# Keeping the split-off low parts of the projection weights in DRAM between the two halves of a decoder layer

## Chip, cores and metric

The kernel runs on one core of a Trainium2 chip. A core has five engines, each with an instruction queue that runs in order: TensorE (PE: matmuls; its weight loads, PEld, are listed apart), VectorE (DVE), ScalarE (ACT), GpSimd (POOL) and SyncE (SP), which here only issues DMAs. The engines wait for each other through semaphores. The time is the device time of one launch in microseconds (us), the median of the runs.

## What is computed

One decoder layer on 1024 tokens of 1024 channels, in float32. What matters here is the first step: the normalised input is multiplied with one wide weight matrix, and its columns feed two mixers.

```python
h = _rms_norm(x, norm_pre_mix[i])
...
p = h @ w_in.astype(h.dtype)
u = p[..., :GLU_COLS]
q = p[..., GLU_COLS:]
q = q + (_token_shift(q) - q) * mu.astype(h.dtype)
...
y = _wkv7(r_h, decay.reshape(B, T, H, N), k_h, v_h, -kk, kk * a_h)
...
c = u[..., :D_CONV] * jax.nn.sigmoid(u[..., D_CONV:])
c = _causal_dwconv(c, cconv_w, cconv_b)
c = jax.nn.silu(_layer_norm(c, cln_g, cln_b))
mix = jnp.concatenate([rwkv_out, c], axis=-1) @ w_out.astype(h.dtype)
```

`_wkv7` is a recurrence over the tokens with a state per head (8 heads of 64), `_causal_dwconv` a convolution over 31 tokens. The layer ends with a feed-forward part of 2816 hidden channels.

## The kernel before

**Precision.** TensorE multiplies in a float32 format with fewer bits than float32 (F32R). So that the result is still a float32 one, each operand is split: the high part `hi` is the value cast to F32R, the low part `lo` is the value minus `hi`. A product is then three matmuls: `wh` with `hi`, `wh` with `lo`, `wl` with `hi`. `split` (L155) makes the two parts of a weight: a cast on ScalarE and a subtraction on GpSimd or VectorE (GpSimd up to the last matrix, `low_pool`).

**Two halves.** The mixer runs over the tokens in two halves of 512 (`h` is 0 and 1 in `mixer`, L1073). `project` (L301) makes one block of 128 columns for one half. A block's weights come as two pieces of 128x512 (256 KB). For each piece `weight` (L160) issues a DMA from `w_in` into `wr` (three buffers), lets ScalarE cast it into `wh` (two buffers) and GpSimd subtract into `wl` (two buffers); then twelve matmuls use it. The 20 blocks of `w_in` are made in `rkv_in` (12: r, k and v) and `glu_in` (8: value and gate of the convolution); two narrower ones, `w_wa` and `w_g`, in `wa_in` and `gate_in`. All of it is done once for each half: the weights of the second half are loaded, cast and subtracted again, 40 pieces of `w_in` in each half.

**What surrounds it.** While the projections of one half run, the other work of the mixer goes on: `conv` (L392) adds 31 shifted products per block on VectorE into a PSUM bank (tile `pc`, L401), `conv_norm` (L403) normalises them (L412 to L417 on VectorE, the power of L153 on GpSimd, transposes and a silu, L422), `elementwise` (L426) prepares decay and keys of a quarter of the tokens (L443 to L498 on VectorE and ScalarE), `scores` (L504), `keys`, `inverses`, `merge` and `recurrence` (L669) make the recurrence. Behind the second half's projections come `w_out`, the feed-forward part's norm (`norm_ffn`, L822) and its matmuls.

**What sets the order.** The program is written as streams with priorities; a scheduler lays the instructions of all streams on the five engines before the launch, by its own model of their durations. On the chip each engine follows that order. `high_priority` in `weight` puts the load, the cast and the subtraction ahead of what its stream has pending. All DMAs of the kernel stand in SyncE's one queue.

Of the kernel before, what the change touches and what calls it, by code (L numbers as in the profile page):

```python
# [12 lines left out]
F32 = mybir.dt.float32  # L13
# [8 lines left out]
P = 128  # L22
# [72 lines left out]
class Trunk:  # L95
# [61 lines left out]
        eng = self.nc.gpsimd if pool else self.nc.vector  # L157
        return self.nc.scalar.copy(hi, src), eng.tensor_tensor(lo, src, hi.bitcast(F32), ALU.subtract)  # L158

    def weight(self, src, shape, home=None, held=None):  # L160

        with self.tc.high_priority():
            raw = (self.f2p.tile(shape, F32, tag="f2", name=self.nm("wr")) if held is self.hp else
                   self.wp.tile(shape, F32, tag="wr", bufs=3, name=self.nm("wr")))
            self.nc.sync.dma_start(raw, src)
            if held:
                hi, lo = self.pair("w", held)
            elif home:
                hi, lo = (home[0].tile(shape, F32R, tag=t, bufs=BUFS[t], name=self.nm("wm")) for t in home[1:])
            else:  # L170
                hi, lo = (self.wp.tile(shape, F32R, tag=t, bufs=2, name=self.nm(t)) for t in ("wh", "wl"))
            self.low = self.split(hi, lo, raw, self.low_pool)[1]
        return hi, lo


    def setup(self):
        nc, tc, ctx, a = self.nc, self.tc, self.ctx, self.a
        pool = lambda name, **kw: ctx.enter_context(tc.tile_pool(name=name, bufs=1, **kw))
        self.cp = pool("const")
        self.small = ctx.enter_context(tc.tile_pool(name="small", bufs=4))  # L180
        self.wp = ctx.enter_context(tc.tile_pool(name="wp", bufs=1))
        self.hp = ctx.enter_context(tc.tile_pool(name="hp", bufs=2 * KT))
        self.dp = pool("dram", space=DRAM)
        self.rowp = pool("rowp")
        cp = self.cp
        self.params = cp.tile([P, NPAR], F32, name="params")
        self.const = cp.tile([P, NCONST], F32, name="const")
        with self.stream("first"):
            nc.sync.dma_start(self.const[:, :P], a["consts"][:, :P])
        nc.sync.dma_start(self.params, a["params"])  # L190
        nc.sync.dma_start(self.const[:, P:], a["consts"][:, P:])
        self.mhalf = cp.tile([P, 8], F32, name="mhalf")
        nc.gpsimd.memset(self.mhalf, -0.5)
        self.mixd = self.dp.tile([SEQ, D], F32, name="mixd")
        self.early = self.dp.tile([EARLY - KEPT, P, HALF], F32, name="early")
        self.x1d = self.dp.tile([SEQ, D], F32, name="x1d")
        self.ssq = cp.tile([P, 8, 4], F32, name="ssq")
        self.sums = self.dp.tile([4, HT, P, 512], F32, name="sums")
        self.ecarry = cp.tile([P, 2, EARLY, 2], F32, name="ecarry")

# [97 lines left out]
            nc.vector.tensor_scalar(row[1], row[1], ss[:, 3:4], None, ALU.mult)  # L298


    def project(self, src, m, hs, halves=False):  # L301


        ps = self.bank()
        if halves:
            ws = [self.weight(src[j], [P, 4, m]) for j in range(2)]
            for ts in (slice(0, 256), slice(256, 512)):
                for k in range(KT):
                    (wh, wl), (hi, lo) = ws[k // 4], hs[k]
                    self.mm(ps[:m, ts], wh[:, k % 4], hi[:, ts], start=k == 0, stop=False)  # L310
                    self.mm(ps[:m, ts], wh[:, k % 4], lo[:, ts], start=False, stop=False)
                    self.mm(ps[:m, ts], wl[:, k % 4], hi[:, ts], start=False, stop=k == KT - 1)
            return ps
        for j in range(2):
            wh, wl = self.weight(src[j], [P, 4, m])
            for kk in range(4):
                hi, lo = hs[4 * j + kk]
                first, last = j == 0 and kk == 0, j == 1 and kk == 3
                self.mm(ps[:m], wh[:, kk], hi, start=first, stop=False)
                self.mm(ps[:m], wh[:, kk], lo, start=False, stop=False)  # L320
                self.mm(ps[:m], wl[:, kk], hi, start=False, stop=last)
        return ps
# [32 lines left out]
    def rkv_in(self, h, hs, st, name):  # L355
        name, pp = name
        j = "rkv".index(name)
        if name == "v":
            t = self.tl("v", [P, 2, HALF])
        else:  # L360
            t = self.row("row", 4).rearrange("p (l t) -> p l t", l=2)
        for l in range(2):
            i = 4 * j + 2 * pp + l
            ps = self.project(self.a["w_in"][i], P, hs, h == 0 and name == "k" and pp == l == 0)
            self.shift(ps, t[:, l], POFF["mu_r"] + i, h)
        st[name, pp] = t

    def glu_in(self, h, hs, st, i):

        nc, a = self.nc, self.a  # L370
        ps2 = self.project(a["w_in"][16 + i], P, hs)
        c = self.tl("c", [P, CONV_W - 1 + HALF])
        with self.tc.high_priority():
            nc.scalar.activation(c[:, CONV_W - 1:], ps2, AF.Tanh, scale=0.5)
        ps1 = self.project(a["w_in"][12 + i], P, hs)
        if h == 0:
            nc.gpsimd.memset(c[:, :CONV_W - 1], 0.0)
        else:
            nc.gpsimd.tensor_copy(c[:, :CONV_W - 1], self.ccarry[:, i])
        with self.tc.high_priority():  # L380
            if h == 0 and i == 3:

                t = self.tl("t2", [P, HALF])
                nc.scalar.copy(t, ps1)
                ps1 = t
            nc.vector.scalar_tensor_tensor(c[:, CONV_W - 1:], c[:, CONV_W - 1:], 1.0, ps1, ALU.add, ALU.mult)
        if h == 0:
            nc.gpsimd.tensor_copy(self.ccarry[:, i], c[:, HALF:])
        st["c", i] = c
# [683 lines left out]
    def mixer(self, sts):  # L1073
# [95 lines left out]
        self.R = self.tl("r", [P, NH, CH])  # L1169
        nc.vector.memset(self.R[64:128], 0.0)  # L1170
        project(0, hs, "k0 w k1 r0 r1")
        with self.stream("norm"):
            two = self.tl("mixr", [P, 2, D])
# [3 lines left out]
            with tc.issue_after(self.mark_hi.ins), tc.issue_after(self.mark_lo.ins):  # L1177
                self.norm_rows(rows)
        weave(quarter(0))
        project(0, hs, "v0 v1 g")  # L1180
        prepare(0)
        project(0, hs, "u0 u1")
        conv(0, 0)
        conv(0, 1, W[0].mark)
# [116 lines left out]
```

## Time and profile before

| | us |
|---|---|
| median of 3 runs (1321.29 to 1322.49) | 1321.41 |
| the profiled execution | 1319.54 |
| its span, first to last instruction | 1317.8 |

The mean granted clock of TensorE in the profiled execution is 0.988 of full speed. The page's slices cut the span into 40 of 33 us; a digit is the busy share in tenths:

```profile
PE   6999989999899989999999899999999999999996
DVE  5276998997799979995531364355555438479566
ACT  6553664567755765556642474443333445544451
POOL 4343433343443322444463466676666540000001
DMA  6222211121124351222354765656564433335326
```

The mixer's first half takes about the first 5 slices, the second half the projections of slices 6 to 11 and the work behind them up to slice 19; the rest is the feed-forward part. A busy share says how long an engine works, not who waits for it; who waits is read from the chain of waits and from the idle time that a row of the order in time shows in brackets, with the engine that ended it.

### The profile page before, as it was taken

To read this page: it belongs to the slowest core of one execution; us is meant where nothing else is said; L and a number is where in the kernel's file an instruction comes from. 1 tells how busy PE (TensorE), PEld (TensorE's weight loads), DVE (VectorE), ACT (ScalarE), POOL (GpSimd) and SP (SyncE) were. 2 spreads that over 40 slices of the span, in tenths; PEclk is the share of its full clock that TensorE was granted. 3 is DMA by queue.
4 is the path that set the end of the run, shared out by engine and by line. 5 is a ranking of instruction groups with operands and counts; after the bars stand their busy time and mean duration, and the time that the engine had idled before them with its cause. 6 is when DMAs were issued, how large, how long until landed. Compare 5 with 4: busy or idle time off the path is not lost.

```text
span 1317.8 us, 22852 instructions
## 1 busy us (share of the span) xinstructions
PE 1259.8 (96%) x8580; PEld 1015.9 (77%) x8580; DVE 877.9 (67%) x1520; ACT 680.0 (52%) x1354; POOL 515.3 (39%) x452
## 2 busy tenths in 40 slices
PE   6999989999899989999999899999999999999996
PEld 4777767777679967787789688888888888888884
DVE  5276998997799979995531364355555438479566
ACT  6553664567755765556642474443333445544451
POOL 4343433343443322444463466676666540000001
PEclk9999999999999989999999999999999999999998
DMA  6222211121124351222354765656564433335326
GB/s 216 81 79 63 66 49 49 42 74 57 49 77 105 119 167 46 68 71 67 102 151 134 257 204 186 192 170 207 170 195 145 122 94 112 97 112 160 104 65 207
DMA packets 85647, 155.79 MB, mean 118 GB/s; under 512 B 9280, under 2 KB 15808, under 8 KB 85536
## 3 DMA queue, kind: packets, MB, share of 16 engines
q1 hardware_dynamic: 85536, 154.33, 38.4%
q8 instruction: 67, 1.10, 0.4%
q14 instruction: 44, 0.36, 0.1%
HBM read 129.13 MB, written 25.17 MB: 117 GB/s over the span
## 4 chain that ended last, share of the span: by engine, by line
PE 72%; DVE 15%; ACT 4%; DMA 3%; issue 3%; POOL 2%; SPq 1%; POOLq 0%; ACTq 0%; DVEq 0%
PE pb L131 60%; DVE pc L401 4%; PE pe L131 4%; PE pn L131 3%; PE xs L131 3%; POOL wl L158 1%; DVE dw L578 1%; DMA x<-x1d 1%; ACT wh L158 1%; DVE pt L470 1%; DVE nrow L962 1%; DMA wr<-ffn_up 1%; PE pe L146 1%; DVE kk L471 1%; DVE h L265 1%
## 5 line engine op out<-in xcount | busy, mean ns | idle before, releaser
L158 POOL TENSOR_TENSOR wl<-wr,wh 128x512 fp32r<-128x512 f32 (+1 forms) x280 | 369.9, 1322 | 439.6 <-ACT wh L158 413.1
L131 PE MATMUL pb<-f,wh 128*128 128x512 f32 x1408 | 442.4, 395 | 2.5 <-ACT pb L773 1.8
L158 ACT CAST wh<-wr 128x512 fp32r<-128x512 f32 (+1 forms) x319 | 195.9, 615 | 331.1 <-PE pb L131 171.8
L131 PEld LDWEIGHTS pb<-f,wh 128*128 128x128 f32 x1408 | 263.5, 188 | 61.9 <-ACT pb L773 2.0
L131 PE MATMUL pb<-f,wl 128*128 128x512 f32 x704 | 280.0, 398 | 2.7 <-POOL wl L158 2.7
L131 PE MATMUL pb<-h,wh 128*128 128x512 f32 (+3 forms) x720 | 229.4, 398 | 2.0 <-ACT wh L158 1.4
L879 DVE SCALAR_TENSOR_TENSOR acc<-pb,params,acc 128x511 f32<-128x511 f32 (+1 forms) x128 | 95.4, 745 | 183.5 <-ACT acc L874 123.9
L401 DVE SCALAR_TENSOR_TENSOR pc<-c,params,pc 128x512 f32<-128x512 f32 x232 | 174.0, 750 | 4.7 <-ACT pc L398 0.5
L131 PEld LDWEIGHTS pb<-f,wl 128*128 128x128 f32 x704 | 132.4, 188 | 37.2 <-POOL wl L158 6.6
L131 PEld LDWEIGHTS pb<-h,wh 128*128 128x128 f32 (+2 forms) x720 | 131.7, 188 | 34.3 <-ACT wh L158 3.3
L131 PE MATMUL pb<-h,wl 128*128 128x512 f32 (+3 forms) x360 | 146.2, 406 | 3.0 <-POOL wl L158 2.9
L153 POOL TENSOR_TENSOR ss<-var,mhalf 128x1 f32<-128x1 f32 x16 | 11.0, 694 | 230.1 <-DVE ss L943 203.3
L131 PE MATMUL pb<-w,a 128*128 128x512 f32 x366 | 89.8, 393 | 0.0
L131 PEld LDWEIGHTS pb<-h,wl 128*128 128x128 f32 (+2 forms) x360 | 67.8, 188 | 22.2 <-POOL wl L158 5.6
L131 PE MATMUL pb<-wh,a 128*128 128x512 f32 x240 | 81.5, 396 | 0.0
L131 PEld LDWEIGHTS pb<-w,a 128*128 128x128 f32 x366 | 68.7, 188 | 16.1
L879 DVE SCALAR_TENSOR_TENSOR pt<-pb,params,pt 128x511 f32<-128x511 f32 (+1 forms) x48 | 35.7, 744 | 33.7 <-ACT ecarry L876 33.2
L919 POOL TENSOR_TENSOR b<-b,b 128x512 f32<-128x512 f32 x44 | 57.1, 1298 | 0.9
L131 PEld LDWEIGHTS pb<-wh,a 128*128 128x128 f32 x240 | 45.1, 188 | 10.6
L874 ACT ACTIVATE acc<-pb,params 128x512 f32<-128x512 f32 x64 | 49.5, 774 | 1.8 <-PE pb L131 1.8
L131 PE MATMUL pb<-wl,a 128*128 128x512 f32 x120 | 47.7, 397 | 0.0
L158 DVE TENSOR_TENSOR a<-act,a 128x512 fp32r<-128x512 f32 x50 | 33.3, 687 | 18.4 <-ACT a L158 18.3
(300 smaller groups left out, 2017.0 us busy)
## 6 DMA issues: line engine op xcount, KB each, us to landing
wr<-ffn_up SPq DMA_DIRECT2D x176, 256.0 KB, 2.7
wr<-w_in SPq DMA_DIRECT2D x80, 256.0 KB, 2.6
b<-ffn_down SPq DMA_DIRECT2D x44, 256.0 KB, 3.9
sums<-b SPq DMA_DIRECT2D x44, 256.0 KB, 2.7
wr<-sums SPq DMA_DIRECT2D x44, 256.0 KB, 2.7
wr<-ffn_down SPq DMA_DIRECT2D x33, 256.0 KB, 2.7
wr<-w_out SPq DMA_DIRECT2D x32, 256.0 KB, 2.7
mixd<-t SPq DMA_DIRECT2D x16, 256.0 KB, 3.2
```

The source lines that it names most:

```text
L131: return self.nc.tensor.matmul(out, lhsT, rhs, start=start, stop=stop, skip_group_check=skip)
L146: self.nc.tensor.transpose(out, in_, self.con("ident")[:n, :n])
L158: return self.nc.scalar.copy(hi, src), eng.tensor_tensor(lo, src, hi.bitcast(F32), ALU.subtract)
L265: self.mark_lo = nc.vector.scalar_tensor_tensor(lo[:, toks], pv, g, hi[:, toks].bitcast(F32), ALU.mult, ALU.subtract)
L401: nc.vector.scalar_tensor_tensor(out, c[:, j:j + HALF], w(j), acc, ALU.mult, ALU.add)
L470: nc.vector.tensor_tensor_scan(sg[:, l], self.con("scan"), sg[:, l], 0.0, ALU.mult, ALU.add)
L471: nc.vector.scalar_tensor_tensor(kk[:, l], k[:, l], self.par("k_k", 2 * pp + l), kk[:, l], ALU.mult, ALU.mult)
L578: nc.vector.tensor_tensor(dv[:, j + 1:, :j], dv[:, j + 1:, :j], tv, ALU.add)
L874: nc.scalar.activation(acc, ps, AF.Identity, scale=w(2), bias=self.par("fb", ch))
L879: nc.vector.scalar_tensor_tensor(acc[:, o:], ps[:, :HALF - o], w(j), acc[:, o:], ALU.mult, ALU.add)
L919: sub = lambda o, x, y, op=ALU.subtract: nc.gpsimd.tensor_tensor(o, x, y, op)
L962: nc.vector.tensor_tensor(out, a, b, op)
```

## The change

`weight` gets a further argument, `kept`: a flag for the half, and a place in a new DRAM tensor `lows` (20 blocks of two pieces). In the first half it works as before, and then a DMA stores the low part into `lows`. In the second half ScalarE still casts the high part out of the loaded `wr`, but the low part comes by a DMA from `lows` into `wl`, and GpSimd's subtraction is left out. `w_wa` and `w_g` stay as they were, and so do all other weights. The low parts are the same bits as before.

```diff
-    def weight(self, src, shape, home=None, held=None):
+    def weight(self, src, shape, home=None, held=None, kept=None):
...
-            self.low = self.split(hi, lo, raw, self.low_pool)[1]
+            if kept and kept[0]:
+                self.nc.scalar.copy(hi, raw)
+                self.nc.sync.dma_start(lo.bitcast(F32), kept[1])
+            else:
+                self.low = self.split(hi, lo, raw, self.low_pool)[1]
+        if kept and not kept[0]:
+            self.nc.sync.dma_start(kept[1], lo.bitcast(F32))
         return hi, lo
...
+        self.lows = self.dp.tile([20, 2, P, 4, P], F32, name="lows")
...
-    def project(self, src, m, hs, halves=False):
+    def project(self, src, m, hs, halves=False, kept=None):
...
+        low = lambda j: kept and (kept[0], self.lows[kept[1], j])
...
-            ws = [self.weight(src[j], [P, 4, m]) for j in range(2)]
+            ws = [self.weight(src[j], [P, 4, m], kept=low(j)) for j in range(2)]
...
-            wh, wl = self.weight(src[j], [P, 4, m])
+            wh, wl = self.weight(src[j], [P, 4, m], kept=low(j))
...
-            ps = self.project(self.a["w_in"][i], P, hs, h == 0 and name == "k" and pp == l == 0)
+            ps = self.project(self.a["w_in"][i], P, hs, h == 0 and name == "k" and pp == l == 0, (h, i))
...
-        ps2 = self.project(a["w_in"][16 + i], P, hs)
+        ps2 = self.project(a["w_in"][16 + i], P, hs, kept=(h, 16 + i))
...
-        ps1 = self.project(a["w_in"][12 + i], P, hs)
+        ps1 = self.project(a["w_in"][12 + i], P, hs, kept=(h, 12 + i))
```

The scheduler lays the whole program anew. SyncE's queue had 573 rows and has 653, GpSimd's had 453 and has 413. Three places follow; the numbers in the names are the buffers', and lines from L158 on stand up to nine lines later in the changed kernel.

SyncE, in the second half's projections of the convolution's blocks (about 317 to 340 us of the profile before), before: one load of a raw piece after the other.

```order
L165 DMA wr_3461<-w_in 128x512
L165 DMA wr_3479<-w_in 128x512
L165 DMA wr_3500<-w_in 128x512
L165 DMA wr_3518<-w_in 128x512
L165 DMA wr_3539<-w_in 128x512
L165 DMA wr_3557<-w_in 128x512
```

The same pieces in the changed kernel, with the loads of low parts between them:

```order
L166 DMA wr_3502<-w_in 128x512
L175 DMA wl_3466<-lows 128x512
L166 DMA wr_3520<-w_in 128x512
L166 DMA wr_3541<-w_in 128x512
L175 DMA wl_3484<-lows 128x512
L175 DMA wl_3505<-lows 128x512
L166 DMA wr_3559<-w_in 128x512
L175 DMA wl_3523<-lows 128x512
L166 DMA wr_3580<-w_in 128x512
L175 DMA wl_3544<-lows 128x512
L166 DMA wr_3598<-w_in 128x512
L175 DMA wl_3562<-lows 128x512
```

A piece's low part (`wl_3523` belongs to `wr_3520`) stands behind the raw load of the piece two to three later. In the first half the stores stand in the same way, each behind the raw load of a piece three or four later.

GpSimd, about 325 to 349 us, before: `XG` is the recurrence's, `mv` and `gn` are powers of the two normalisations.

```order
L158 TENSOR_TENSOR wl_3482<-wr_3479,wh_3481 128x512
L691 TENSOR_TENSOR XG_3855<-r_3788,GE_1163 64x256
L153 TENSOR_TENSOR mv_3203<-var_3205,mhalf 128x1
L158 TENSOR_TENSOR wl_3503<-wr_3500,wh_3502 128x512
L158 TENSOR_TENSOR wl_3521<-wr_3518,wh_3520 128x512
L153 TENSOR_TENSOR gn_3694<-var_3700,mhalf 128x8
L158 TENSOR_TENSOR wl_3542<-wr_3539,wh_3541 128x512
L691 TENSOR_TENSOR XG_3858<-r_3788,GE_1163 64x256
L158 TENSOR_TENSOR wl_3560<-wr_3557,wh_3559 128x512
L153 TENSOR_TENSOR mv_3226<-var_3228,mhalf 128x1
```

The same stretch in the changed kernel:

```order
L700 TENSOR_TENSOR XG_3896<-r_3829,GE_1188 64x256
L153 TENSOR_TENSOR mv_3244<-var_3246,mhalf 128x1
L153 TENSOR_TENSOR gn_3735<-var_3741,mhalf 128x8
L700 TENSOR_TENSOR XG_3899<-r_3829,GE_1188 64x256
L153 TENSOR_TENSOR mv_3267<-var_3269,mhalf 128x1
```

The subtractions are gone and the rest keeps its order.

VectorE, about 353 to 360 us, before: scores (L525, L526), the recurrence's sum (L710) and the last tile of the convolution's normalisation (L412 to L417).

```order
L525 TENSOR_TENSOR l_590_3721<-pe_3724,const 128x4x64
L526 TENSOR_TENSOR ca_3722<-pe_3724,const 128x4x64
L710 TENSOR_TENSOR r_3846<-xs_94,XG_3855 64x256
L710 TENSOR_TENSOR r_3846<-xs_95,XG_3858 64x256
L412 BN_STATS bs_3247<-pc_3242 128x6
L725 TENSOR_REDUCE gn_3899<-mixr_1959 128x8
L414 BN_AGGR mv_3249<-bs_3247 128x2
L386 SCALAR_TENSOR_TENSOR c_3536<-c_3536,pb_3538 128x512
```

And in the changed kernel, from the same score on:

```order
L534 TENSOR_TENSOR l_590_3762<-pe_3765,const 128x4x64
L535 TENSOR_TENSOR ca_3763<-pe_3765,const 128x4x64
L719 TENSOR_TENSOR r_3887<-xs_95,XG_3896 64x256
L395 SCALAR_TENSOR_TENSOR c_3577<-c_3577,pb_3579 128x512
L534 TENSOR_TENSOR l_590_3762<-pe_3779,const 128x4x64
L535 TENSOR_TENSOR ca_3778<-pe_3779,const 128x4x64
L534 TENSOR_TENSOR l_590_3762<-pe_3780,const 128x4x64
L535 TENSOR_TENSOR ca_3778<-pe_3780,const 128x4x64
L719 TENSOR_TENSOR r_3887<-xs_96,XG_3899 64x256
L421 BN_STATS bs_3288<-pc_3283 128x6
```

The gate's product (L386) and the next four score products now stand ahead of the normalisation's last tile. Up to here VectorE's order is that of before; from here on it differs in several places, up to about 640 us.

## Prediction

> **What bounds the kernel now.** I read the page's busy shares and slices first, then the chain of waits cut into stretches, then the waits by engine, and last the order in time of the stretch where the removed work lies.
>
> ```profile
> PE 1259.8 (96%) x8580; PEld 1015.9 (77%) x8580; DVE 877.9 (67%) x1520; ACT 680.0 (52%) x1354; POOL 515.3 (39%) x452
> PE 72%; DVE 15%; ACT 4%; DMA 3%; issue 3%; POOL 2%; SPq 1%; POOLq 0%; ACTq 0%; DVEq 0%
> L158 POOL TENSOR_TENSOR wl<-wr,wh 128x512 fp32r<-128x512 f32 x40 | 54.0, 1352 | 89.4 <-ACT wh L158 74.2 <-PE pb L131 8.6 <-ACT r L700 3.4
> ```
>
> TensorE sets the time: 96% busy, 72% of the chain. GpSimd is 39% busy, on 2% of the chain. The third row is what the change takes away: 40 subtractions of 1.352 us, 54.0 us on GpSimd, counted in the stretch 181 to 380 us where the second half's projections run. An engine with 2% of the chain cannot return 54 us. The question is where those 40 held somebody else.
>
> ```profile
> 181.00:312.00 131.00, 125.63 (x1352) 97.26 (x1346) 120.38 (x209) 72.14 (x144) 47.07 (x45) 0.97 0.19 52
> 312.00:362.00 50.00, 45.98 (x363) 35.44 (x362) 37.01 (x66) 40.30 (x83) 22.18 (x22) 1.00 0.18 52
> 362.00:460.00 98.00, 93.99 (x1026) 83.22 (x1025) 93.16 (x162) 60.03 (x127) 38.13 (x32) 0.98 0.36 98
> by line: PE pb L131 58.0%; PE pe L131 13.5%; PE xs L131 10.1%; DVE pc L401 5.2%; PE pe L146 3.3%; DVE h L265 2.5%; PE xs L146 1.8%; PE Y L131 1.6%; DVE l L495 0.8%; DVE pt L494 0.8%; DVE pt L498 0.6%; DVE l L489 0.5%; PE pb L146 0.5%; DVE c
> by line: PE pb L131 36.2%; issue 8.3%; PE pe L131 7.0%; ACT co L422 5.6%; POOL wl L158 5.6%; PE xs L131 4.2%; ACT wh L158 3.8%; PE pc L146 3.7%; ACT kk L448 3.2%; ACT L422 2.6%; ACT L473 2.6%; ACT L474 2.6%; ACT pt L492 2.2%; ACT pt L465 1.
> by line: DVE pc L401 30.9%; PE pb L131 8.7%; DVE dw L578 5.6%; issue 5.3%; DVE m L158 4.8%; DVE t L767 3.2%; DVE v L335 2.6%; DVE sub L576 2.6%; DVE pt L470 2.3%; DVE l L534 2.3%; DVE dw L567 2.2%; DVE l L590 2.1%; DVE pt L468 2.0%; DVE kk
> ```
>
> The first three rows give busy time of PE, PEld, DVE, ACT, POOL in three stretches; the next three are the chain's shares in the same stretches. From 181 to 312 the chain is TensorE's own work, so freeing GpSimd there returns almost nothing. From 312 to 362 it passes from TensorE to ScalarE, VectorE and GpSimd, and TensorE stands idle for 4 of 50 us: this is the only stretch where the low parts are on the chain. From 362 to 460 VectorE is 95% busy and is the chain; it starts when the stretch before ends, so a gain made by 362 is carried on.
>
> **The removed subtractions.** They cost in two ways: TensorE waits for a low part, and VectorE is held while GpSimd subtracts.
>
> ```profile
> PEld pb L131 <- POOL wl L158: 1.8, 2, 1.1
> PE pb L131 <- POOL wl L158: 0.9, 2, 0.6
> L401 DVE SCALAR_TENSOR_TENSOR pc<-c,params,pc 128x512 f32<-128x512 f32 x91 | 68.4, 752 | 2.0
> L498 DVE SCALAR_TENSOR_TENSOR pt<-row,params,pt x16: 472/485/1519, 76.1 to 463.2; 128x256 f32<-128x256 f32 x16
> 325.25 1.71 POOL L158 TENSOR_TENSOR wl<-wr,wh 128x512 fp32r<-128x512 f32 x1 [6.01 <-ACT wh L158]
> 326.34 1.16 DVE L489 SCALAR_TENSOR_TENSOR l<-kk,pt 128x512 f32<-128x512 f32 x1
> 325.13 0.69 DVE L488 SCALAR_TENSOR_TENSOR kk<-pt,kk 128x512 f32<-128x512 f32 x1
> 330.47 2.71 POOL L158 TENSOR_TENSOR wl<-wr,wh 128x512 fp32r<-128x512 f32 x2
> 331.26 2.20 DVE L498 SCALAR_TENSOR_TENSOR pt<-row,params,pt 128x256 f32<-128x256 f32 x2
> 335.21 0.63 ACT L473 ACTIVATE pt<-pt 128x512 f32<-128x512 f32 x1 [2.29 <-DVE pt L470]
> 343.44 0.50 PE L131 MATMUL pb<-h,wl 128*128 128x512 f32 x1 [0.63 <-POOL wl L158]
> ```
>
> Waits first: in the whole stretch TensorE's matmuls wait 0.9 us for low parts and its weight loads 1.8, partly the same time. Then holding: the convolution's step at L401, which adds into PSUM, takes 752 ns throughout, but L498, with two SBUF operands, takes 485 at the median and up to 1519 ns. Both long cases in 330 to 335 lie inside GpSimd's pair of subtractions.
>
> The Trainium skill, page "SBUF — State Buffer", section "SBUF: two separate sides", says that VectorE and GpSimd share one port pair under an exclusive lock, and that only VectorE operations with two SBUF inputs or in a two-port mode are caught. By that rule the 68.4 us of L401 gain nothing from an idle GpSimd, and the trace agrees with its steady 752 ns; if every VectorE step were slowed, the sum below would be several times larger.
>
> *Term 1, 325 to 344 us.* L489 takes 1.16 us where its neighbour of the same shape, L488, takes 0.69: 0.47 lost. The two L498 take 2.20 where two medians make 0.97: 1.23 lost. Together 1.70 us, ahead of the scan L470 for which ScalarE waits 2.29 us, so ScalarE gets all of it. Its in-order work then leads to the cast for which TensorE waits (next fence), and TensorE's wait of 0.63 us for that piece's low part goes too: 2.33 us.
>
> ```profile
> 338.98 0.44 PE L146 MATMUL pc<-const,co 128*128 128x128 f32 x2 [0.72 <-ACT co L422]
> 339.87 0.66 PE L146 MATMUL pe<-const,mixr 128*128 128x128 f32 x4 [0.46 <-DVE mixr L731]
> 342.08 0.73 PE L131 MATMUL pb<-h,wh 128*128 128x512 f32 x2 [0.44 <-ACT wh L158]
> 349.64 0.63 PE L146 MATMUL pc<-const,t 128*128 128x128 f32 x4 [0.80 <-DVE t L417]
> 344.99 1.91 DVE L498 SCALAR_TENSOR_TENSOR pt<-row,params,pt 128x256 f32<-128x256 f32 x2
> 345.26 1.36 POOL L158 TENSOR_TENSOR wl<-wr,wh 128x512 fp32r<-128x512 f32 x1 [0.85 <-ACT wh L158]
> ```
>
> TensorE cannot gain more than it idles: 0.72+0.46+0.44+0.63 = 2.25. Term 1 is **-2.2 us**. *Term 2, 345 to 350:* the second pair of L498 loses 1.91-0.97 = 0.94 us under the subtraction at 345.26, ahead of the normalisation's power on GpSimd and of L417, for which TensorE idles 0.80 us. Term 2 is **-0.8 us**. What is late next there is ScalarE (40.30 of 50 us busy, with its table loads) and TensorE's own pace.
>
> **The added loads (second half).** Each low part now comes by one more 256 KB DMA, started when its buffer is let go, which is when TensorE is done with the piece two before.
>
> ```profile
> wr<-w_in SPq DMA_DIRECT2D x80, 256.0 KB, 2.6
> sums<-b SPq DMA_DIRECT2D x44, 256.0 KB, 2.7
> mixd<-t SPq DMA_DIRECT2D x16, 256.0 KB, 3.2
> x<-x1d SPq DMA_DIRECT2D x16, 256.0 KB, 4.3
> 40.89 16.16 PE pb L131 x71
> 52.37 1.30 POOL L158 TENSOR_TENSOR wl<-wr,wh 128x512 fp32r<-128x512 f32 x1 [1.43 <-ACT wh L158]
> 55.09 1.29 POOL L158 TENSOR_TENSOR wl<-wr,wh 128x512 fp32r<-128x512 f32 x1 [1.42 <-ACT wh L158]
> SPq L165 <- POOL wl L158: 341.6, 94, 15.1
> ```
>
> Undisturbed, TensorE takes 16.16/71 = 0.228 us for a matmul, 2.73 us for a piece's 12; the low part is first needed by the third matmul, 0.46 us in. So a load has 2.73+0.46 = 3.2 us even when pieces follow without a gap, and lands in 2.6 plus some 0.2 to start: 0.4 us to spare. Over 181 to 380 us the 40 pieces of GpSimd's row above take 199/40 = 5.0 us each, and there is 2 us more. Cost: **0**; with the 3.2 us of the mixd row the tight pieces would be 0.2 late, with 4.3 us 1.3 late, and if ten of the 40 were that tight (an estimate; the mean has 2 us more), +13 us. Behind a waiting low-part load on SyncE's queue stands the raw load of three or four pieces later; before, that load waited for GpSimd's subtraction (SyncE's row: 341.6 us of such waits), and now for ScalarE's cast, which comes earlier. The 80 new issues fall into those 341.6 us.
>
> **The added stores (first half).** A store stands behind the raw load that waited for the same subtraction, so its own wait is over when it is reached; nothing new blocks SyncE. What is new: the buffer cannot take the subtraction two pieces on until the store has landed. In the tightest flow two subtractions start 2.72 us apart (52.37, 55.09). A buffer's round is the subtraction 1.29, the issue of load and store about 0.45, the landing L, and 0.1 to wake: under 2 x 2.73 = 5.46 us as long as L is below 3.6. With 2.7 (the row of stores of the same size, sums) it is 4.5. Cost: **0**; with 4.3 us a piece takes (1.84+4.3)/2 = 3.07 instead of 2.73, +0.34 us for each of at most 40 pieces, +13.6 us.
>
> The Trainium skill, page "DMA: Bandwidth & Descriptors", section "Anatomy of one DMA — SWDGE (gpsimd) path", puts a DMA at about 2.0 us plus its bytes over 436 GB/s, an estimate of 2.6 us here, but warns of a surprisingly long completion when the target is HBM. It speaks against the stores; the sums row (2.7 us, stored to DRAM) shows no such delay at this size, and by its long case the sum would be the rival of the stores below.
>
> **The order.** Up to about 340 us VectorE, ScalarE and TensorE keep their order but for one small exchange; behind that the scheduler has laid convolution normalisation, scores and the feed-forward norm anew. Nothing in the trace prices that: I bound it by the four score products moved ahead of the normalisation (4 x 0.41 us by the first L525 row below, with its wait of 1.23) to 2.9 us either way, and take 0.
>
> ```profile
> 352.12 0.42 DVE L525 TENSOR_TENSOR l<-pe,const 128x256 f32<-128x256 f32 x1 [1.23 <-PE pe L131]
> L331 DVE SCALAR_TENSOR_TENSOR row<-carry,params,row 128x1 f32<-128x1 f32 x8 | 4.4, 549 | 1.0 <-ACT row L329 0.9
> L331 DVE SCALAR_TENSOR_TENSOR row<-carry,params,row x8: 207/262/1249, 206.5 to 282.1; 128x1 f32<-128x1 f32 x8
> ```
>
> **Sum.** -2.2 - 0.8 + 0 + 0 + 0 = -3.0 us. The profiled execution took 1319.54 us (span 1317.8 and 1.7 around it), so 1316.5 by its own time; the median of the runs shown, 1321.41, is 1.87 above it, which gives **1318.4 us**.
>
> **Rivals.**
> - *Hidden anyway (no change).* TensorE's idle time in 312 to 362 is refilled by the next waits, ScalarE's table loads and the new order; only the waits for low parts, 0.9 us, return: 1320.5. For it: five engines meet there. Against: ScalarE's 2.29 us of waiting leaves room.
> - *VectorE's relief counts everywhere (faster).* L331's eight steps lose (549-207) x 8 = 2.7 us between 206 and 282; if this, and the 0.9 us, came through beside the 3.0, and the new order helped by another 1 us: -7.6, 1313.8. For it: VectorE is 92% busy there (120.38 of 131). Against: the chain there is TensorE's.
> - *The stores throttle the first half (slower).* If a store lands in over 3.6 us, GpSimd waits for it at every piece of the dense flow, behind it all it does. At 4.3 us: +0.34 us for some 16 dense pieces (an estimate), +5.4, and -3.0 kept for half: 1325.3. For it: x1d's row. Against: the sums row, and DMA shares of 0.2 to 0.3 there.
> - *The new order loses* its 2.9 us and the second pair of TensorE's waits stays (0.8): 1318.4+3.7 = 1322.1, no change that can be told.
> - *That the subtractions are not gone* can be left out: the order shows 40 of them missing on GpSimd.
>
> **How the numbers follow.** A measurement of this kernel tells about 0.2%, 2.6 us, from no change. Forecast 0.45 (of it 0.35 faster by more than that, 0.10 within); hidden 0.15 and the lost order 0.08, both within; everywhere 0.14, faster; the stores 0.12, and late loads or an order that loses more, 0.06, slower. Faster 0.49, same 0.33, slower 0.18. The range goes from 1311.5 (everywhere, with the order's 2.9 in place of 1) to 1325.5 (the stores), leaving out about 2 in 10.
>
> **What would show it.** Right: the pairs of L498 near 330 and 345 at 0.97 us; no wait of TensorE for low parts in the second half; L470 to L473 without 2 us of ScalarE idle; stores landing in under 3.6 us; the stretch that VectorE fills begins about 3 us earlier. Wrong: GpSimd waiting for stores between 29 and 170 us, TensorE waiting for loads of low parts, or a begin of that stretch where it was.

## The result, and the profile after

| | us | runs |
|---|---|---|
| before, median | 1321.35 (1315.26 to 1322.49) | 6 |
| changed, median | 1310.36 (1308.80 to 1312.54) | 6 |
| ratio | 0.9916, 95% interval 0.9900 to 0.9932 | |
| profiled execution, before and changed | 1319.54 and 1310.48 | |

The change makes the kernel 11 us faster, 0.8%. The forecast was 3 us. A second set of runs of the changed kernel (e15) gave 0.9927, interval 0.9908 to 0.9946; the mean granted clock of its runs was 0.9845, and so was that of the runs of before beside them, so the gain is not a matter of the clock.

First the page's busy shares and the chain of the changed kernel, then the busy times of PE, PEld, DVE, ACT and POOL, the granted clock, the DMA share and GB/s in the three stretches that the prediction read:

```profile
PE 1260.4 (96%) x8580; PEld 1018.6 (78%) x8580; DVE 864.0 (66%) x1520; ACT 678.4 (52%) x1354; POOL 462.6 (35%) x412
PE 77%; DVE 14%; ACT 4%; DMA 2%; issue 2%; POOL 1%; SPq 0%; POOLq 0%; ACTq 0%; DVEq 0%
181.00:312.00 131.00, 127.63 (x1368) 98.95 (x1362) 115.92 (x210) 72.16 (x144) 13.56 (x21) 0.95 0.33 102
312.00:362.00 50.00, 48.85 (x381) 37.90 (x381) 32.67 (x68) 41.33 (x85) 8.56 (x12) 1.00 0.37 113
362.00:460.00 98.00, 92.72 (x1066) 82.45 (x1062) 91.77 (x162) 60.35 (x130) 33.57 (x29) 0.98 0.37 112
```

GpSimd lost 52.7 us of work and VectorE, whose instructions are the same 1520, lost 13.9 us of busy time. TensorE is as busy as before (1260.4 against 1259.8 us) in a span that is 9.1 us shorter, so the gain is TensorE's idle time. In 312 to 362 us it now idles for 1.15 us where it idled for 4.02.

The places of the two terms, in order of time (start, duration, engine, line, operation, wait and what ended it). Lines are 9 higher than before: L498 here is L489 of before, L507 is L498, L482 is L473.

```profile
326.37 0.67 DVE L498 SCALAR_TENSOR_TENSOR l<-kk,pt 128x512 f32<-128x512 f32 x1
330.81 0.87 DVE L507 SCALAR_TENSOR_TENSOR pt<-row,params,pt 128x256 f32<-128x256 f32 x2
333.43 0.63 ACT L482 ACTIVATE pt<-pt 128x512 f32<-128x512 f32 x1 [0.48 <-DVE pt L479]
334.95 0.19 PEld L131 LDWEIGHTS pb<-h,wl 128*128 128x128 f32 x1 [0.21 <-DMA wl<-lows]
342.72 0.88 DVE L507 SCALAR_TENSOR_TENSOR pt<-row,params,pt 128x256 f32<-128x256 f32 x2
```

This is as forecast: 1.16 became 0.67, the pairs 2.20 and 1.91 became 0.87 and 0.88, and ScalarE's wait of 2.29 became 0.48. The fourth row is the only place where TensorE's side waits for one of the loads, for 0.21 us (0.65 us at the same place in e15's profile).

The new DMAs and one of the old stores (KB of each, median us from issue to landing), the GpSimd subtractions that are left, with what ended the idle time before them, and VectorE's convolution step (L401 of before):

```profile
lows<-wl SPq DMA_DIRECT2D x40, 256.0 KB, 3.2
wl<-lows SPq DMA_DIRECT2D x40, 256.0 KB, 2.6
sums<-b SPq DMA_DIRECT2D x44, 256.0 KB, 2.4
L158 POOL TENSOR_TENSOR wl<-wr,wh 128x512 fp32r<-128x512 f32 x232 | 308.8, 1332 | 334.1 <-ACT wh L158 311.5 <-PE pb L131 8.6 <-DMA lows<-wl 5.1
L410 DVE SCALAR_TENSOR_TENSOR pc<-c,params,pc 128x512 f32<-128x512 f32 x232 | 174.1, 751 | 8.3 <-ACT pc L407 4.4
```

The loads land in 2.6 us, as taken. The stores land in 3.2 us rather than 2.7 (the slowest in 4.5), and GpSimd waits for them four times in the first half, 8.2 us in all: 5.1 us ahead of full pieces, as the row says, and 3.1 ahead of a narrower one. This hardly reached TensorE: up to the 1001st matmul it takes 158.5 us before and 158.8 changed.

**Where the 11 us came from.** The same matmuls can be compared in stretches. Of TensorE's 8580 matmuls in order of time I take those behind which both orders have issued the same set: the 1001st (167 us before), 2001st (259), 2714th (346), 3484th (428), 4762nd (540) and 5601st (655). A stretch is the difference of two such starts:

```
stretch of before, us    before   changed   changed (e15)
167 to 259                 91.9      91.8      91.1
259 to 346                 87.5      85.0      85.1
346 to 428                 82.3      81.4      80.0
428 to 540                111.4     107.1     109.8
540 to 655                115.0     114.4     112.8
655 to the last matmul    649.9     649.6     650.3
```

The forecast's first term lies in the second row, its second (345 to 350 us) at that row's end and just behind it: the row is 2.5 us shorter. But some 6 us more came between 346 and 655 us, mostly behind 428, where the change removes nothing. There the program differs only in the order of its instructions.

### The profile page after: what moved, and what is told of

It reads as the page before. It is cut to its first block, busy times and chain, and to the rows that moved or that the text cites. A ratio compares the mean times of both kernels' runs of the same rounds, so it can differ in the third digit from the quotient of the medians.

```text
span 1308.7 us, 22940 instructions
## 1 busy us (share of the span) xinstructions
PE 1260.4 (96%) x8580; PEld 1018.6 (78%) x8580; DVE 864.0 (66%) x1520; ACT 678.4 (52%) x1354; POOL 462.6 (35%) x412
## 4 chain that ended last, share of the span: by engine, by line
PE 77%; DVE 14%; ACT 4%; DMA 2%; issue 2%; POOL 1%; SPq 0%; POOLq 0%; ACTq 0%; DVEq 0%
PE pb L131 63%; PE pe L131 5%; DVE pc L410 4%; PE pn L131 3%; PE xs L131 3%; DVE dw L587 1%; PE pe L146 1%; DMA x<-x1d 1%; DVE pt L479 1%; DVE nrow L971 1%; DMA pt<-mixd 1%; DVE kk L480 1%; POOL wl L158 1%; PE pc L146 0%; DVE m L158 0%
## 5 line engine op out<-in xcount | busy, mean ns | idle before, releaser
L158 POOL TENSOR_TENSOR wl<-wr,wh 128x512 fp32r<-128x512 f32 (+1 forms) x240 | 316.3, 1319 | 360.9 <-ACT wh L158 332.4
L158 ACT CAST wh<-wr 128x512 fp32r<-128x512 f32 (+1 forms) x279 | 171.5, 615 | 296.0 <-PE pb L131 142.3
L131 PE MATMUL pb<-wh,a 128*128 128x512 f32 x240 | 81.5, 396 | 0.0
L700 POOL TENSOR_TENSOR XG<-r,GE 64x256 f32<-64x256 f32 x30 | 20.8, 696 | 85.5 <-DVE r L719 80.8
```

Source lines behind the costliest of these rows:

```text
L131: return self.nc.tensor.matmul(out, lhsT, rhs, start=start, stop=stop, skip_group_check=skip)
L700: nc.gpsimd.tensor_tensor(x[64:128], R[64:128, gs], w.GE[64:128, c, gs].unsqueeze(2).broadcast_to([64, 4, CH]), ALU.mult)
```

## The experiments

The order can be held apart from the work. In the kernels below each engine's instructions are tied, by order alone, each to the one ahead of it in a list. The profile of e3, tied to the order of before, shows TensorE, VectorE, ScalarE and GpSimd with the same instructions in the same order as the profile of before. What the list doesn't have (a store, a load) stands behind the same neighbour as in the schedule that the work would get by itself.

```diff
         self.ffn_down(acts)
+        self.pin()
...
+    def pin(self):
...
+            want = [made[d + n] for n, d in enumerate(table[name])]
+            for a, b in zip(want, want[1:]):
+                self.tc.add_manual_dep(
+                    b, a.name, mybir.DependencyInfo(mybir.DependencyClass.NoSync, mybir.DependencyReason.DATA),
+                    reason="pinned")
```

All of them are timed against the kernel before on the same chip, with 6 to 12 runs of each and 23 to 29 of before. The ratio is this run's time over that of before. "Early" is the order up to 445 us, "late" behind it; old is the order of before, new that of the changed kernel.

| run | work | early | late | median, us | before, us | ratio, 95% interval |
|---|---|---|---|---|---|---|
| e1 | change | old | old | 1315.87 | 1321.66 | 0.9951 (0.9933 to 0.9969) |
| e10 | change | old | old | 1317.66 | 1320.32 | 0.9970 (0.9954 to 0.9986) |
| e8 | change | new | old | 1317.49 | 1322.35 | 0.9959 (0.9944 to 0.9974) |
| e9 | change | old | new | 1311.75 | 1320.32 | 0.9928 (0.9906 to 0.9950) |
| e15 | change | new | new | 1311.02 | 1321.63 | 0.9927 (0.9908 to 0.9946) |
| e2 | before | new | new | 1318.41 | 1321.66 | 0.9974 (0.9958 to 0.9990) |
| e6 | before | old | new | 1317.01 | 1322.35 | 0.9950 (0.9931 to 0.9970) |
| e7 | before | old | new to 525 us only | 1320.63 | 1322.35 | 0.9993 (0.9973 to 1.0012) |
| e11 | before | old | new from 530 us only | 1319.90 | 1320.32 | 0.9994 (0.9980 to 1.0009) |
| e13 | change | old | new to 525 us only | 1316.55 | 1321.63 | 0.9963 (0.9946 to 0.9980) |
| e14 | change | old | new from 530 us only | 1315.93 | 1321.63 | 0.9963 (0.9947 to 0.9978) |
| e3 | stores alone | old | old | 1322.81 | 1321.66 | 1.0003 (0.9988 to 1.0017) |
| e4 | 4 blocks kept | old | old | 1319.44 | 1321.66 | 0.9979 (0.9965 to 0.9993) |
| e5 | other 16 blocks | old | old | 1322.85 | 1322.35 | 1.0006 (0.9991 to 1.0021) |
| e12 | 5 blocks kept | old | old | 1317.71 | 1320.32 | 0.9979 (0.9965 to 0.9994) |

**Work and order apart: e1 and e2.**

> The change's work, with every engine's instructions held in the order that they had before (the added loads and stores stand where the change's own schedule has them, behind the same neighbour). Theory A, the forecast (own terms, -2.2 and -0.8; the new order is worth nothing): -3 us against before, about 1318.4, which would leave the change's measured -11 unexplained. Theory B (own terms -3, the new order another -5 to -8): -3 here too, about 1318, and the rest must show in the run of before's work in the new order. Theory C (the lighter work gives all of it, the order only follows): -9 to -11 here, 1310 to 1312. A and B part from C here, A from B in the next run.

> The work of before (GpSimd subtracts in both halves, nothing is stored or loaded), with every engine's instructions held in the order of the changed kernel. Theory A: 0 within the 2.9 us that the forecast gave the order. Theory B: -5 to -8, 1313 to 1316, with the gain between 455 and 640 us after the start. Theory C: 0 or slower, since an order made for lighter work does not suit the old work.

Each alone gives a part: by the medians -5.8 us for the work in the old order and -3.3 for the old work in the new order, against -11.0 for both. So theory C falls (the old work gains by the order). Theory A, by which the order is worth nothing within 2.9 us, is not refuted by e2 alone, whose interval is -1.3 to -5.6 us; e6 below goes beyond it. B stands in kind, but neither of its sizes was met: it had -3 for e1 and -5 to -8 for e2. The next runs give the work alone less than e1 did (e10) and show where the order pays.

**The stores, and parts of the work: e3, e4, e5, e12.** e3 replaces the second half's load by the subtraction of before and keeps the stores; e4, e5 and e12 keep the low parts of some blocks only.

```diff
-            if kept and kept[0]:
-                self.nc.scalar.copy(hi, raw)
-                self.nc.sync.dma_start(lo.bitcast(F32), kept[1])
-            else:
-                self.low = self.split(hi, lo, raw, self.low_pool)[1]
+            self.low = self.split(hi, lo, raw, self.low_pool)[1]
```

```diff
+U23 = (14, 15, 18, 19)
...
-        low = lambda j: kept and (kept[0], self.lows[kept[1], j])
+        low = lambda j: (kept[0], self.lows[kept[1], j]) if kept and kept[1] in U23 else None
```

> Only the stores of the first half are added to the kernel before; the second half subtracts as before and does not load what was stored; order of before. Forecast's term for the stores: 0 (a store lands in under 3.6 us). The rival of the stores: +5.4 or more, with GpSimd waiting for stores between 29 and 170 us.

> The low parts are kept for four of the 20 blocks only, those whose subtractions fall into about 309 to 347 us (8 of 40 pieces); order of before. Forecast: terms 1 and 2 lie here, so nearly all of -3 us. Rival (VectorE's relief counts everywhere): about a fifth of what e1 gives.

> The counterpart of e4: the low parts are kept for the other 16 blocks (32 of 40 pieces), the four blocks around 309 to 347 us subtract as before; order of before. Forecast: 0, its terms lie in e4's four blocks. The theory that the rest of e1 comes from here: e1 less e4, about -3 (1318.5), of it 0.9 from two VectorE operations near 183 to 186 us that take 1.11 and 1.13 us before and 0.68 after; if that is all, -0.9, which these rounds cannot tell from 0.

> e4's four blocks and the first block of the second half (its subtractions at 182 and 184 us), 10 of 40 pieces; order of before. If the work's own gain lies in these two places only: e4's -2.8 and 0.9 more, -3.7, about as e1. If the other 30 pieces count as well: e4's value, and e1 stays lower.

The stores cost nothing that can be measured (+0.4 us by the ratio, within -1.6 and +2.2 by the interval), and the rival of the stores falls. The four blocks around 309 to 347 us give -2.8 us (by ratio), close to the forecast's -3.0; the other 32 pieces give nothing that can be told (+0.8, -1.2 to +2.8). With the first block added (e12) the ratio is the same as e4's, so the 0.9 us expected there can't be told by the time. The stretches tell it. In all seventeen profiles, 259 to 346 us takes 87.4 to 87.5 us where those four blocks subtract and 85.0 to 85.1 where their low parts are loaded. From the 1001st matmul to the 1233rd (167 to 191 us before) it is 24.3 to 24.6 us where the first block subtracts and 23.5 to 23.7 where it loads: 0.8 us that the forecast had not counted. Before, in order of time:

```profile
182.25 1.33 POOL L158 TENSOR_TENSOR wl<-wr,wh 128x512 fp32r<-128x512 f32 x1 [1.30 <-PE pb L131]
184.01 1.27 POOL L158 TENSOR_TENSOR wl<-wr,wh 128x512 fp32r<-128x512 f32 x1 [0.44 <-ACT wh L158]
183.02 1.11 DVE L494 TENSOR_TENSOR pt<-pt,row 128x512 f32<-128x512 f32 x1
184.71 1.13 DVE L495 TENSOR_TENSOR l<-pt,pt 128x512 f32<-128x512 f32 x1
190.71 0.69 PE L146 MATMUL pe<-const,mixr 128*128 128x128 f32 x2 [2.49 <-DVE h L265]
```

Changed, the same three instructions of VectorE and TensorE:

```profile
183.29 0.68 DVE L503 TENSOR_TENSOR pt<-pt,row 128x512 f32<-128x512 f32 x1
184.56 0.68 DVE L504 TENSOR_TENSOR l<-pt,pt 128x512 f32<-128x512 f32 x1
190.11 0.69 PE L146 MATMUL pe<-const,mixr 128*128 128x128 f32 x2 [0.93 <-DVE h L273]
```

Two VectorE steps with two SBUF operands lose 0.43 and 0.45 us under GpSimd's subtractions. VectorE then works without a gap up to the normalisation for which TensorE waits at 190 us, so the 0.88 us reach TensorE: with this block's low parts loaded, the matmul behind that wait starts 0.85 to 0.87 us earlier, counted from 180 us, in the kernels that have the order of before. (The wait itself falls by more, from 2.49 to 0.93, because TensorE's granted clock is 0.50 from 187 us on in the changed profile and 1.00 before, so that its own work ahead of the wait takes longer.)

**The late order: e6, e7, e8, e9, and e10 to e15.**

> The work of before, in the order of before up to 445 us and from there in the order of the changed kernel. Theory B' (the new order pays behind 445 us whatever the work is, and costs the old work some 4 us between 353 and 420 us): about -4.4 in TensorE's idle time, 1317, and better than e2. Theory C (order only follows the lighter work): 0. If e2's gain is chance, this shows 0 as well.

> As e6, but only the stretch from 445 to 525 us has the new order; behind it the order of before again. Theory B': -2.8, the part of e6 in which TensorE's waits for VectorE around 475 to 504 us go (2.02 us at 503.9 among them); the other 1.6 of e6 belong to the feed-forward part behind 525 us.

> The change's work, in the changed kernel's own order up to 445 us and from there in the order of before. Theory B': the changed kernel loses what the late order gave, +4.4 against it, so about 1315 (-6 against before). Theory C: stays near 1310.

> The change's work, in the order of before up to 445 us and from there in the changed kernel's order: the fourth cell beside e1, e8 and the changed kernel. Theory B' (the late order is worth the same with either work): e1 less the 4.4 to 6.6 that e6 showed, 1309.5 to 1311.5, level with the changed kernel or a little better. If the late order needs the early one: as e1, 1316.

> e1 once more. e4 and e5 split its work and gave -2.8 and +0.5, while e1 gave -5.8 in its medians, with a higher mean granted clock (0.9873 against 0.9843 of before). If that clock was chance, this run gives -2 to -4; if it belongs to the work, -6 again, at a clock of 0.987 or more.

> As e6, but the new order starts only at 530 us, in the feed-forward part. By TensorE's idle time (6.3 us behind 521 us before, 4.7 in the changed kernel): -1.6. By the medians of e6 less e7 (1317.0 against 1320.6): -3.6.

> The change's work in the order of before, but for the stretch from 445 to 525 us, which has the changed kernel's order. By TensorE's idle time -2.8 against e1 and e10 (median of both some 1316.8), so 1314. If the stretch gives the whole late gain: 1311, level with e9. If it gives nothing: 1316 to 1317.

> The change's work in the order of before up to 530 us and in the changed kernel's order behind it. By TensorE's idle time -1.6 against e1 and e10, so 1315. If the feed-forward part gives the whole late gain: 1311. If nothing: 1316 to 1317.

> The changed kernel itself, beside the two: -11 again, 1310, with TensorE idle some 9 us less than before in its profile.

The late new order pays with either work: -6.6 us for the old work (e6, by ratio), and for the change's work -9.5 (e9) against -6.5 and -4.0 for the same work in the old order (e1, e10). Given back (e8), it costs the changed kernel 4 to 6 us. The early new order shows no gain that the times can tell: e8 has -5.4 where e1 and e10 have -6.5 and -4.0, and e9 has -9.5 where e15 has -9.6.

For the halves of the late order no gain can be told either: e7, e11, e13 and e14 are level with what they started from, before or e1 and e10, by their intervals. But the intervals of e7 and e11 reach down to -3.6 and -2.6 us, so the -2.8 and -1.6 that I had priced by TensorE's idle time are not excluded.

e10 is the same kernel as e1: by the medians the work alone in the old order is worth 5.8 us in one and 2.7 in the other. The expectation of e10 had named the clock, and that e1's was high by chance fits what came: the runs of e1 had a mean granted clock of 0.9873 beside 0.9843 of before, those of e10 0.9863 beside 0.9851. The runs of e8 had 0.9883 beside 0.9847, so the clock is not why e8 is slower than the changed kernel.

The stretches again, now as means over all profiles of a kind (number of profiles in brackets). In the early stretches the old work in the old order is before, e3, e6, e7 and e11, the change in the old order e1, e9, e10, e13 and e14, the change in the new one the changed kernel, e8 and e15, and the old work in the new one e2. In the late stretches before, e1, e3, e4, e5, e10 and e12 have the old order, and the changed kernel, e2, e6, e9 and e15 the new one:

```
early          old work, old order (5)   change, old order (5)   change, new order (3)   old work, new order (1)
167 to 259              92.4                     90.2                    91.4                     91.9
259 to 346              87.5                     85.0                    85.1                     87.5
346 to 428              83.8                     83.7                    81.0                     86.0

late           old order (7)   new order (5)   new to 525 only: e7, e13   new from 530 only: e11, e14
428 to 540        111.7            108.1           108.7    109.6             111.1    111.3
540 to 655        115.0            113.5           115.0    117.1             114.3    114.5
```

(e4, e5 and e12, with a part of the work, are left out of the early means. e8, which goes back to the old order at 445 us, is left out of the late ones: it took 114.1 and 115.0.) By these means the changed kernel gains 1.0 + 2.4 + 2.8 in the early part and 3.6 + 1.5 in the late one: 11.3 us, and 11.0 were measured. The work in the old order gains 2.2 + 2.5 + 0.1 = 4.8.

**The clock inside the stretches.** These means hold some chance. In every profile TensorE's granted clock drops to 0.50 for about 3.4 us, or for two to four times as long, and where it does differs between runs of the same instructions: in e1 it does so from 342.9 us on, in e10 not between 198 and 398 us, and the matmuls there cost e1 1.5 us more. Rows of busy time for the stretch 540 to 655 us, with the granted clock behind POOL's count: before, e15, the changed kernel, 3.4 us inside that same stretch of the changed kernel, e11 and e13.

```profile
539.80:654.80 115.00, 112.38 (x840) 88.81 (x839) 86.74 (x134) 72.86 (x153) 52.85 (x44) 1.00 0.26 76
532.20:645.00 112.80, 110.64 (x847) 88.92 (x841) 87.90 (x138) 74.51 (x156) 52.88 (x44) 1.00 0.27 77
532.20:646.60 114.40, 112.26 (x850) 90.09 (x844) 87.94 (x138) 74.62 (x156) 52.72 (x44) 0.99 0.26 76
634.20:637.60 3.40, 3.40 (x10) 2.63 (x9) 0.03 (x1) 2.13 (x3) 0.57 (x1) 0.50 0.50 154
541.80:656.10 114.30, 112.15 (x850) 90.00 (x843) 86.99 (x135) 74.52 (x156) 52.77 (x44) 0.99 0.28 76
534.00:651.10 117.10, 112.86 (x841) 88.69 (x840) 90.23 (x137) 74.06 (x155) 52.45 (x44) 1.00 0.28 76
```

With the clock full throughout, every profile of the old order takes 115.0 us here, and the new order 112.8 to 112.9 (e2, e9, e15). With 3.4 us at half clock the new order takes 114.4 and 114.5 (the changed kernel, e6), and so do e11 and e14 with 114.3 and 114.5, which have it from 530 us only. So in this stretch the new order is worth 2.1 to 2.2 us, also without the part ahead of it; in the means, and in e11 and e14 above all, the time at half clock hides it. In 428 to 540 us the time at half clock is 3.4 to 10.2 us. With 10.2 the old order takes 111.0 to 113.0 us and the new one 109.7 (e15); with 6.8 it is 111.2 and 111.6 (e4, e12) against 107.1 and 108.5 (the changed kernel, e6). So the late order is worth some 3.5 to 6.5 us by the profiles, and 6.6 by e6's ratio.

The early rows say less than their means. In 167 to 259 us the change in either order takes 89.3 us with 6.8 us at half clock (e1, e14), 90.6 to 91.0 with 10.2 (e9, e10, e13) and 91.1 to 91.8 with 13.7 (the changed kernel, e8, e15): the difference of 1.2 us between the two orders goes with the clock. In 346 to 428 us, with 3.4 us at half clock, the changed kernel and e8 take 81.4 and 81.5 us, e1, e10 and e13 82.5 to 83.3, of which TensorE waits 1.0 to 1.9 for one low part (last section). The old work in the new order is one profile alone (e2, 86.0 us against 82.2 to 85.5), so that the new order costs the old work time there is not shown.

The work alone is best read where the clock is full. By the starts of the same matmuls in kernels with the order of before, 0.85 to 0.87 us come at 190 us, and 2.6 to 2.7 us between 259 and 355 us (e4, e10, e13): 3.5 us together, between the 2.7 and 5.8 that e10 and e1 gave by their medians.

What the new order does late can be seen around 500 us, where the second half's norm in front of the feed-forward (pb<-kk,row are TensorE's scaled transposes, L265, now L273, VectorE's low parts f) meets the inverses of the last quarter (L576 and L578, now L585 and L587). Before:

```profile
500.53 0.69 DVE L556 TENSOR_TENSOR pt<-pe,v 128x512 f32<-128x512 f32 x1
501.32 0.68 DVE L556 TENSOR_TENSOR pt<-pe,v 128x512 f32<-128x512 f32 x1
501.93 0.68 DVE L727 TENSOR_TENSOR mixr<-mixr,gn 128x512 f32<-128x512 f32 x1
502.89 0.87 DVE L265 SCALAR_TENSOR_TENSOR f<-pb,params,f 128x256 fp32r<-128x256 f32 x2
503.90 3.18 PE L131 MATMUL pb<-kk,row 128*128 128x128 f32 x16 [2.02 <-DVE sub L576]
507.31 1.00 PE L131 MATMUL pb<-f,wh 128*128 128x512 f32 x2 [0.22 <-DVE sub L576]
```

Changed:

```profile
498.15 0.48 DVE L273 SCALAR_TENSOR_TENSOR f<-pb,params,f 128x256 fp32r<-128x256 f32 x1
498.55 0.68 DVE L736 TENSOR_TENSOR mixr<-mixr,gn 128x512 f32<-128x512 f32 x1
499.15 0.48 DVE L273 SCALAR_TENSOR_TENSOR f<-pb,params,f 128x256 fp32r<-128x256 f32 x1
499.54 0.68 DVE L565 TENSOR_TENSOR pt<-pe,v 128x512 f32<-128x512 f32 x1
499.77 0.70 PE L131 MATMUL pb<-f,wh 128*128 128x512 f32 x2 [0.61 <-DVE f L273]
```

Before, VectorE takes two products of L556 and the group norm's L727 first, then the f that reads a bank of TensorE's products out; TensorE waits 2.02 us, until that f is done (502.89 + 0.87 = 503.76), with 16 transposes still to come, and the feed-forward's first product starts at 507.31. In the changed kernel the two kinds alternate, and that product starts at 499.77, 7.5 us earlier, in a run that is some 4 to 5 us ahead at that point. About 1 us of that is the clock: in before it is at half from 504.5 us on, and the 16 transposes take 3.18 us where the changed kernel's take 1.05 for the last eight. (The profile names L576, VectorE's next step, as the releaser of the 2.02 us.) That the f is late because of the order is read from these rows; it was not tried by itself.

## Why the prediction was wrong

The sign was right and the time 8 us too high, 1.1 us beyond the range. (By its own terms the low end of the range is 1311.9, not 1311.5: 3.0, 2.7, 0.9 and 2.9 off 1321.4.)

- **The step that failed: "The order. ... I bound it ... to 2.9 us either way, and take 0."** The bound came from the one move that I had priced, four score products at 353 to 360 us. But the order differs up to 640 us, through the stretch in which TensorE idles most between 20 and 655 us: 10.0 us between 428 and 540 us before. The late order alone, with the old work, is worth 6.6 us by e6 (4.0 to 9.1 by the interval), and some 3.5 to 6.5 by the stretches. Both are beyond the 2.9 us at which I had bounded it. What the early order is worth, the runs can't tell.
- **"From 181 to 312 the chain is TensorE's own work, so freeing GpSimd there returns almost nothing"** was wrong by 0.85 us, at one place. The chain's share is a mean over 131 us; inside it TensorE waited 2.49 us at 190.71, behind VectorE. The rival in which VectorE's relief counts everywhere took its 2.7 us from L331, around which TensorE does not wait (no wait of 0.1 us or more between 200 and 290 us before), and so named the right effect at the wrong place.
- **Terms 1 and 2, -2.2 and -0.8:** the sum of 3.0 was nearly right, its division was not. e4 gave -2.8, and L489, L498 and L473 changed as forecast. By the starts of the same matmuls (e4, e10, e13) 2.8 us are gained up to 344.5 us, and 0.1 of them is lost again by 355 us. So term 1 was too small: what TensorE idles by the rows, 2.25 us, was no upper bound for what it can gain. And term 2 came to nothing: the wait of 0.80 us for L417 is gone, but just ahead of it TensorE's wait for ScalarE's `mixr` (L740) grew from 0.67 to 1.22 us.
- **The stretch that VectorE fills** starts 3.0 us earlier, by the starts of TensorE's matmuls between 360 and 400 us. This too was as forecast; what came later was not.
- **The stores, 0:** right in the time (e3), though the way there was looser than thought: 3.2 us to land, with 8.2 us of GpSimd waiting, which the forecast had listed as a sign of trouble. The page's slices show GpSimd at three to four tenths there, so it has room to wait.
- **The loads, 0:** right; TensorE's side waited for one of 40, for 0.21 us (0.65 in e15).
- **The Trainium skill's lock** of VectorE and GpSimd ("SBUF — State Buffer", section "SBUF: two separate sides") held: L401, which adds into PSUM, took 752 ns in the prediction's row (750 over the whole run) and has a mean of 751 changed, while VectorE as a whole lost 13.9 us of busy time.
- **The Trainium skill's warning** of long completions towards HBM ("DMA: Bandwidth & Descriptors", section "Anatomy of one DMA — SWDGE (gpsimd) path") is not borne out as a rule here. That section is about DMAs issued from GpSimd, and here SyncE issues them all. Of two stores of 256 KB to DRAM in the changed kernel, lows<-wl takes 3.2 us to land and sums<-b 2.4, and the load of the same size 2.6.

What stays open: how the gain of the late order divides between its halves, since the times of e7, e11, e13 and e14 don't separate theirs from chance; why e13 takes 117.1 us behind its seam at full clock, where e7 takes 115.0; and some 1 to 4 us of the 11 that lie between the work's 3.5 and the late order's share, for which the early order and chance are the candidates.

## What to carry to other kernels

Where a scheduler lays the instructions again, the new order is a term of its own, and its size is to be judged by the idle time of the bounding engine in all of the re-laid stretch, not by the one move that can be priced. To tell work from order, hold the order and change the work, and the other way round. And a share of the chain over 100 us says nothing of a single wait inside it: list the waits of the bounding engine one by one, and ask of each what its releaser was held by. And before a difference of 2 us between two profiles is explained, compare the granted clock in that stretch.

## What the runs showed of the hardware

The hold between VectorE and GpSimd goes both ways, and which engine is held differs between runs of the same instructions. e1 and e14 have the same instructions in the same order up to 530 us. In e1, GpSimd and TensorE:

```profile
394.18 4.15 POOL L221 TENSOR_TENSOR wl<-wr,wh 128x512 fp32r<-128x512 f32 x1 [6.75 <-ACT wh L221]
394.86 1.88 DVE L221 TENSOR_TENSOR m<-co,m 128x512 fp32r<-128x512 f32 x3
398.38 0.50 PE L194 MATMUL pb<-wl,m 128*128 128x256 f32 x2 [1.87 <-POOL wl L221]
```

and in e14:

```profile
395.04 1.59 POOL L221 TENSOR_TENSOR wl<-wr,wh 128x512 fp32r<-128x512 f32 x1 [6.74 <-ACT wh L221]
395.61 1.10 DVE L650 TENSOR_TENSOR dw<-dw,sub 128x56 f32<-128x56 f32 x1
397.92 1.81 POOL L221 TENSOR_TENSOR wl<-wr,wh 128x512 fp32r<-128x512 f32 x1 [1.28 <-ACT wh L221]
```

In e1 VectorE's subtractions, also of two SBUF operands, run at full speed (three in 1.88 us), and GpSimd's takes 4.15 us where the one behind it takes 1.28; TensorE waits 1.87 us for it. In e14 GpSimd's two take 1.59 and 1.81 us, VectorE's step of 56 elements takes 1.10 instead of 0.20, and TensorE does not wait there. The profile of before that the forecast was worked out from has no such wait either, nor has e7, while e6 and e11, the same instructions up to that point, have it with 0.89 and 1.88 us. Such holds and the times at half clock put a stretch of one profile up to 3 us off another of the same instructions: 346 to 428 us takes 82.2 to 85.5 us in the five profiles of the old work in the old order. The longest, e7's, has no such wait, but 10.4 us at half clock where before has 3.4.
